# Rebuilding the head of a transformer-block kernel: modulation vector in column quarters, head 0's v, k, q accumulated feature by feature, one gate projection moved forward

## The chip, the cores and the metric

The kernel runs on one core of a Trainium2 chip. The metric is the device time of the whole program in microseconds (us), a median over runs. The engines are named as the profile names them: PE (TensorE; PEld is its weight load), DVE (VectorE), ACT (ScalarE), POOL (GpSimd) and SP (SyncE, which issues most DMAs).

## The reference

One layer of a diffusion block on 512 latent tokens and 256 context tokens, width 1024, one batch, all in float32. The core of it:

```python
mod_lat = jnp.split(jax.nn.silu(c) @ w_ada[l] + b_ada[l], 6, axis=-1)
mod_ctx = jnp.split(jax.nn.silu(c_ctx)[None, :] @ w_ada[l] + b_ada[l], 6, axis=-1)
...
pl = project(modulate(rmsnorm(x, g_mix[l]), sh1, sc1), w_in[l], w_dec_up[l], b_dec[l])
pc = project(modulate(rmsnorm(ctx, g_mix[l]), sh1c, sc1c), w_in[l], w_dec_up[l], b_dec[l])
o_c, s_cf, s_cb = gla_bidir(pc[0], pc[1], pc[2], pc[4], pc[5], zeros_state, zeros_state)
o_l, _, _ = gla_bidir(pl[0], pl[1], pl[2], pl[4], pl[5], s_cf, s_cb)
mix_l = merge_branches(o_l, pl[3], ...)          # o * silu(g), convolution branch, output projection
x = x + gt1[:, None, :] * mix_l
x = x + gt2[:, None, :] * swiglu(modulate(rmsnorm(x, g_ffn[l]), sh2, sc2), w_ffn_in[l], w_ffn_out[l])
return rmsnorm(x, g_final)
```

`project` multiplies by one matrix `w_in` whose columns are q, k (512 each), v, g (1024 each), a 32-column low-rank input `dd` for the decays, and the columns of the convolution and of the branch gates. There are 4 attention heads with 128 key and 256 value channels each. The change concerns the first of these steps: `mod` (shift and scale of the first norm, 2048 of the 6144 columns of `w_ada`), the modulated tokens, and the projections of head 0.

## The kernel before

Matmuls keep float32 accuracy by splitting each operand into a rounded part (`hi`) and the rest (`lo`) and adding three products; that is `mm3`, and L145 is the line on which all such matmuls are recorded. `split` makes the two parts: ACT casts `hi`, DVE subtracts for `lo`. The helper `Pinned` (L103) records most ACT and DVE work. A weight piece is loaded raw by SP's queue (tag `raw`, 4 buffers), then split.

PSUM has 8 banks: 3 are handed out as `bank`, 5 as `gbank`; a new tile of a name waits for the oldest one of its kind to be read out.

**The head before.** The modulation is a matrix-vector product for two vectors at once (`c2v`, latent and context). It is made in 8 pieces, one per 128-column feature tile f: shift and scale columns of f, so 256 output columns, stationary operand 2 columns wide, 8 float32 products over k, each of which the engine runs as two instructions of 256 columns (L279). For f = 3 and 6 (`ADA_SPLIT`) the weights are split first (L274). A row of 2 results is copied to SBUF, turned into columns by tiny matmuls (`adac`, L298), biased (`modT`, `gs`), and the feature of the normalised, transposed tokens is scaled and split (`mod_split`, L288 to L290). Tokens are normalised and transposed through PSUM (L251 to L261) between the pieces. Once all eight features exist, head 0's v is computed for the four latent token tiles (v, 256 columns, and dd, 32), then context tiles, k, the decays' inputs (`ddt`, z), q.

**The order.** Up to `pinned[0] = True` a scheduler orders the instructions of each engine from its own estimates; behind it, program order holds. From there on the numbers and letters of ORDER0, ORDER and ORDER3 set how many steps of filler matmuls stand between the attention steps of a head: `fill(n)` issues n steps. Heads 0 to 2 use the next head's v, k and q as filler; head 3 uses the g and branch-gate projections of all heads (`G_ORDER`). Each step is one mm3. `SPLITS` and `SPLITS3` are the step numbers at which the next weight unit is split and another one's load issued.

Of the kernel before, what the change touches and what calls it, by code (L numbers as in the profile page):

```python
# [23 lines left out]
H = 4  # L24
# [22 lines left out]
def hybrid_block(ctx: ExitStack, tc: tile.TileContext, x, c, ctxt, c_ctx, w_ada, b_ada, g_mix, w_in,  # L47
# [15 lines left out]
    ADA_SPLIT = (3,6)  # L63
# [79 lines left out]

    def mm(*a, **k):
        pin(nc.tensor.matmul(*a, **k))  # L145

    def tr(*a):
        pin(nc.tensor.transpose(*a))
# [18 lines left out]
    w_ada_v = w_ada[:, :2 * D].rearrange("(q a p) (s f) -> q p a s f", q=2, p=P, s=2)  # L167

    def ada_load(f):
        us = []  # L170
        for q in range(2):
            u = wp.tile([P, 4, 2, P], F32, tag="raw", name=f"r_wa{f}_{q}", bufs=4)
            for s_ in range(2):
                nc.sync.dma_start(u[:, :, s_, :], w_ada_v[q][:, :, s_, f * P:(f + 1) * P])
            us.append(u)
        return us

    wa = {0: ada_load(0)}
    ident = cst.tile([P, P], F32, name="ident")
    make_identity(nc, ident)  # L180
    eps = cst.tile([P, 1], F32, name="eps")
# [32 lines left out]
    c2v = c2.rearrange("p (s k) -> p k s", s=2)  # L214

    c4 = cst.tile([P, KT, 4], F32R, name="c4")
    nc.vector.tensor_copy(c4[:, :, 0:2], c2v)
    nc.vector.tensor_sub(c4[:, :, 2:4], c2v, f32(c4)[:, :, 0:2])
    sel = cst.tile([4, 2], F32, name="sel")
    nc.vector.tensor_add(sel, ident[0:4, 0:2], ident[0:4, 2:4])  # L220


    vrow = u2("vrow")
    vec = cst.tile([P, R_N], F32, name="vec")

    def small_vectors():
        for r0, src in ((R_GM, g_mix), (R_GF, g_ffn), (R_BA, b_ada), (R_GH, g_head)):
            n = src.shape[1] // P
            nc.sync.dma_start(vrow[r0:r0 + n, :P], src.rearrange("o (r f) -> (o r) f", f=P))
        nc.sync.dma_start(vrow[R_BD:R_BD + 8, :P], b_dec[0].rearrange("d (r f) -> (d r) f", f=P))  # L230
        nc.sync.dma_start(vrow[R_WC:R_WC + 24, :P], w_conv[0].rearrange("d (r f) -> (d r) f", f=P))
        vps = bank("vps")
        nc.tensor.transpose(vps[:, :R_N], vrow[:R_N, :P], ident[:R_N, :R_N])
        nc.vector.tensor_copy(vec, vps[:, :R_N])


    hp = tc.alloc_tile_pool(name="hp", bufs=1)
    xsT = hp.tile([P, KT, T], F32, name="xsT")
    xcT = hp.tile([P, KT, TC], F32, name="xcT")

    def tokens(i):
        src, dst, j = (x, xsT, i) if i < NT else (ctxt, xcT, i - NT)
        xt = hp.tile([P, D], F32, tag="xt", name=f"xt{i}", bufs=6)
        if i < NT:
            nc.sync.dma_start(xt, src[j * P:(j + 1) * P, :])
        else:
            with tc.issue_after(v_loads[-1].ins):
                nc.sync.dma_start(xt, src[j * P:(j + 1) * P, :])
        junk = hp.tile([P, D], F32, tag="jk", name=f"junk{i}", bufs=1)
        ss = sm.tile([P, 1], F32, tag="ss", name=f"ss{i}")  # L250
        nc.scalar.activation(junk, xt, AF.Square, accum_out=ss)  # L251
        r = rstd_of(ss, 1, D, f"x{i}")
        nc.vector.tensor_scalar_mul(xt, xt, r)
        for hh_ in range(2):
            tp = gbank(f"xtp{i}_{hh_}", (P, 4, P))
            for k in range(4):
                nc.tensor.transpose(tp[:, k, :], xt[:, (hh_ * 4 + k) * P:(hh_ * 4 + k + 1) * P], ident)
            if hh_ == 0:
                nc.scalar.copy(dst[:, :4, j * P:(j + 1) * P], tp)
            else:  # L260
                nc.vector.tensor_copy(dst[:, 4:, j * P:(j + 1) * P], tp)  # L261
# [3 lines left out]
    rows = {}  # L265

    def ada_rows(f):
        rows[f] = gbank(f"ada{f}")
        if f in ADA_SPLIT:
            for q in range(2):  # L270
                parts_ = split_raw(wa[f][q], f"wa{f}_{q}")
                for i, w_ in enumerate(parts_):
                    for k in range(4):
                        nc.tensor.matmul(rows[f][0:4, :256], c4[:, q * 4 + k, :], w_[:, k].rearrange("p s f -> p (s f)"),  # L274
                                         start=(q + i + k == 0), stop=(q + i == 2 and k == 3))
            return
        for q in range(2):
            for k in range(4):
                nc.tensor.matmul(rows[f][0:2, :256], c2v[:, q * 4 + k, :], wa[f][q][:, k].rearrange("p s f -> p (s f)"),  # L279
                                 start=(q + k == 0), stop=(q == 1 and k == 3))  # L280
# [5 lines left out]
    def mod_split(src, f, j, hi, lo):  # L286
        g_, sh = gs[:, f, j:j + 1], modT[:, f, 0, j:j + 1]
        nc.scalar.activation(hi, src[:, f, :], AF.Identity, scale=g_, bias=sh)  # L288
        nc.vector.tensor_scalar(src[:, f, :], src[:, f, :], g_, sh, ALU.mult, ALU.add)
        nc.vector.tensor_sub(lo, src[:, f, :], f32(hi))  # L290

    def modulate(f):
        n = 4 if f in ADA_SPLIT else 2
        rsb = sm.tile([4, 256], F32, tag="adar", name=f"adar{f}", bufs=2)
        nc.vector.tensor_copy(rsb[0:n, :], rows[f][0:n, :256])
        cp = gbank(f"adac{f}")
        for s_ in range(2):
            nc.tensor.matmul(cp[:, 2 * s_:2 * s_ + 2], rsb[0:n, s_ * P:(s_ + 1) * P], sel[0:n, :], start=True, stop=True)  # L298
        nc.vector.tensor_tensor(modT[:, f], cp[:, 0:4].rearrange("p (s c) -> p s c", s=2),
                                vec[:, R_BA + f:R_BA + f + KT + 1:KT].unsqueeze(2).broadcast_to([P, 2, 2]), ALU.add)  # L300

        nc.vector.scalar_tensor_tensor(gs[:, f, :], modT[:, f, 1, :], 1.0,
                                       vec[:, R_GM + f:R_GM + f + 1].broadcast_to([P, 2]), ALU.add, ALU.mult)
        mod_split(xsT, f, 0, *h[f])
# [16 lines left out]
    ada_rows(0)  # L321
    with tc.issue_after(silu_c.ins):
        tokens(0)
    tokens(1)
    wa[1] = ada_load(1)
    ada_rows(1)
    tokens(2)
    tokens(3)
    small_vectors()
    for f in range(2, KT):  # L330
        wa[f] = ada_load(f)
        ada_rows(f)
        modulate(f - 2)
        if f == 5:
            wdu_load()

# [22 lines left out]
    v_loads = []  # L359
    stv = [u2(f"st{i}", F32, (P, 4, P)) for i in range(2)]  # L360

    def v_slab(hd):

        n = HV + 32
        units = []
        per = 1024 // n
        for k in range(0, KT, per):
            e = min(k + per, KT)
            r = wp.tile([P, e - k, n], F32, tag="raw", name=f"r_v{hd}_{k}", bufs=4)
            nc.sync.dma_start(r[:, :, :HV], w_in[k * P:e * P, CV + hd * HV:CV + (hd + 1) * HV].rearrange("(a p) b -> p a b", p=P))  # L370
# [78 lines left out]


    v_slab(0)
    modulate(KT - 2)
    modulate(KT - 1)
    for i in range(NC_):
        tokens(NT + i)
# [634 lines left out]
```

## Time and profile before

| | before |
|---|---|
| median of 3 runs | 1024.05 us (1023.79 to 1024.25) |
| the profiled execution: its own time | 1025.91 us |
| span of that execution's trace | 1024.2 us |
| PE busy | 1003.4 us, 98% of the span |
| DVE busy | 549.2 us, 54% |
| ACT busy | 384.2 us, 38% |
| DMA, mean over the span | 114 GB/s |

Times in the rows are microseconds from the start of the span. In a row of the timeline or of the grouped view, the text before the arrow is what is written and the text behind it is what is read; x and a number is a count of instructions. Where a mean is given, it is in nanoseconds and is the duration of one instruction; on a pipelined engine neighbours overlap, so the pace of a long run is its length divided by its count.

### The profile page before, as it was taken

To read this page: it belongs to the slowest core of one execution; us is meant where nothing else is said; L and a number is where in the kernel's file an instruction comes from. 1 tells how busy PE (TensorE), PEld (TensorE's weight loads), DVE (VectorE), ACT (ScalarE), POOL (GpSimd) and SP (SyncE) were. 2 spreads that over 40 slices of the span, in tenths; PEclk is the share of its full clock that TensorE was granted. 3 is DMA by queue.
4 is the path that set the end of the run, shared out by engine and by line. 5 is a ranking of instruction groups with operands and counts; after the bars stand their busy time and mean duration, and the time that the engine had idled before them with its cause. 6 is when DMAs were issued, how large, how long until landed. Compare 5 with 4: busy or idle time off the path is not lost.

```text
span 1024.2 us, 13014 instructions
## 1 busy us (share of the span) xinstructions
PE 1003.4 (98%) x5270; PEld 833.4 (81%) x5274; DVE 549.2 (54%) x885; ACT 384.2 (38%) x594; POOL 6.2 (1%) x18
## 2 busy tenths in 40 slices
PE   6999999999999999999999999999999999999997
PEld 3598888888788888888888888888888888888886
DVE  4778876776536687778534445743332333322423
ACT  4547465558344322233123223642332322311223
POOL 2000000000000000000000000000000000000000
PEclk9999999999999999999999999999999999999999
DMA  8932112112326767666623322233233233232302
GB/s 250 272 113 62 41 43 62 35 50 62 104 71 181 211 179 200 196 195 213 199 83 97 106 86 83 83 104 103 82 104 102 83 109 97 84 127 77 124 21 83
DMA packets 117845, 117.16 MB, mean 114 GB/s; under 512 B 5415, under 2 KB 105881, under 8 KB 117785
## 3 DMA queue, kind: packets, MB, share of 16 engines
q1 hardware_dynamic: 117528, 116.07, 37.8%
q8 instruction: 41, 0.67, 0.3%
q0 software_dynamic: 256, 0.26, 0.1%
q14 instruction: 20, 0.16, 0.0%
HBM read 114.22 MB, written 2.10 MB: 114 GB/s over the span
## 4 chain that ended last, share of the span: by engine, by line
PE 92%; DVE 2%; ACT 2%; DMA 1%; issue 1%; SPq 0%; ACTq 0%
PE f L145 23%; PE fo L145 10%; PE v L145 5%; PE yc L145 4%; PE yg L145 4%; PE cb L145 4%; PE g L145 4%; PE ch L145 4%; PE cc L145 4%; PE gb L145 4%; PE ga L145 4%; PE mx L145 3%; PE kl L145 2%; PE o L145 2%; PE F L145 2%; PE q L145 2%
## 5 line engine op out<-in xcount | busy, mean ns | idle before, releaser
L145 PE MATMUL f<-h,h_fa 128*128 128x512 f32 (+1 forms) x384 | 111.0, 372 | 0.2 <-DVE h L103 0.2
L145 PE MATMUL f<-h,h_fb 128*128 128x512 f32 (+1 forms) x384 | 110.3, 372 | 0.0
L145 PEld LDWEIGHTS f<-h,h_fa 128*128 128x128 f32 x384 | 70.2, 188 | 13.3 <-DVE h L103 0.8
L145 PEld LDWEIGHTS f<-h,h_fb 128*128 128x128 f32 x384 | 70.0, 188 | 12.4
L145 PE MATMUL f<-h,l_fb 128*128 128x512 f32 (+1 forms) x192 | 71.3, 371 | 0.0
L145 PE MATMUL f<-h,l_fa 128*128 128x512 f32 (+1 forms) x192 | 71.3, 371 | 0.0
L103 DVE TENSOR_TENSOR l_fa<-r_fa,h_fa 128x1024 fp32r<-128x1024 f32 x22 | 26.9, 1225 | 74.6 <-ACT h_fa L103 74.6
L103 DVE TENSOR_TENSOR l_fo<-r_fo,h_fo 128x1024 fp32r<-128x1024 f32 x22 | 26.9, 1224 | 69.0 <-ACT h_fo L103 69.0
L145 PE MATMUL fo<-h_fo,ah 128*128 128x512 f32 x154 | 60.5, 393 | 0.0
L145 PE MATMUL fo<-l_fo,ah 128*128 128x512 f32 x154 | 60.5, 393 | 0.0
L145 PE MATMUL fo<-h_fo,al 128*128 128x512 f32 x154 | 60.4, 392 | 0.0
L807 DVE SCALAR_TENSOR_TENSOR acc<-r_wa,c,acc 128x256 f32<-128x256 f32 x112 | 54.1, 483 | 5.9 <-DMA r_wa<-in_w_ada_dram 3.0
L145 PE MATMUL v<-h_v,h 128*128 128x256 f32 (+1 forms) x256 | 51.3, 294 | 1.9 <-DVE vl L103 1.7
L103 ACT CAST h_fo<-r_fo 128x1024 fp32r<-128x1024 f32 x22 | 23.1, 1050 | 71.0 <-PE fo L145 27.4
L145 PEld LDWEIGHTS v<-h_v,h 128*128 128x128 f32 x256 | 41.9, 195 | 2.7 <-DVE vl L103 1.9
L145 PEld LDWEIGHTS f<-h,l_fb 128*128 128x128 f32 x192 | 36.2, 188 | 6.2
L145 PEld LDWEIGHTS f<-h,l_fa 128*128 128x128 f32 x192 | 36.1, 188 | 6.2
L145 PE MATMUL g<-h,h_g 128*128 128x512 f32 x128 | 39.9, 392 | 0.0
L145 PE MATMUL gb<-h,h_gb 128*128 128x512 f32 x128 | 39.8, 392 | 0.0
L145 PE MATMUL cb<-h,h_cb 128*128 128x512 f32 x128 | 39.7, 391 | 0.0
L145 PE MATMUL ch<-h,h_ch 128*128 128x512 f32 x128 | 39.6, 390 | 0.0
L145 PE MATMUL cc<-h,h_cc 128*128 128x512 f32 x128 | 39.6, 390 | 0.0
(276 smaller groups left out, 2275.5 us busy)
## 6 DMA issues: line engine op xcount, KB each, us to landing
r_wa<-in_w_ada_dram SPq DMA_DIRECT2D x32, 512.0 KB, 4.7
r_fa<-in_w_ffn_in_dram SPq DMA_DIRECT2D x22, 512.0 KB
r_fb<-in_w_ffn_in_dram SPq DMA_DIRECT2D x22, 512.0 KB, 3.5
r_fo<-in_w_ffn_out_dram SPq DMA_DIRECT2D x22, 512.0 KB, 3.6
r_wa<-in_w_ada_dram SPq DMA_DIRECT2D x32, 256.0 KB, 3.8
r_kq<-in_w_in_dram SPq DMA_DIRECT2D x16, 256.0 KB, 4.6
r_g<-in_w_in_dram SPq DMA_DIRECT2D x8, 512.0 KB, 3.8
r_gb<-in_w_in_dram SPq DMA_DIRECT2D x8, 512.0 KB
```

Source lines behind the costliest of these rows:

```text
L103: return lambda *a, **k: pin(getattr(self.engine, op)(*a, **k))
L145: pin(nc.tensor.matmul(*a, **k))
L807: nc.vector.scalar_tensor_tensor(acc, w_[:, k, :], ck, acc, ALU.mult, ALU.add)
```

## The change

The head is rewritten. The modulation is made in four quarters of two feature tiles each (shift and scale together 512 output columns). Its stationary operand `cw` is now 32 columns wide, 2 used and 30 zero. The eight products over k are spread over four groups of 32 output partitions (`g_ = 32 * (k % 4)`), so the groups sit in different columns of PE's array; `sel` then adds the four groups while it turns rows into columns. No piece is split any more. The loads come in whole 1-KB rows per column block instead of 512-byte rows.

Head 0's weights come in four pieces `w00` to `w03` of 256 input features with v, dd, k and q columns together (1088 values per partition). As soon as a feature tile k is modulated, its products are added to six open accumulators: four token tiles of v in `vo`, k in `ko`, q in `qo` (`gather_v`, `gather`). These hold all 3 `bank` and 3 of the 5 `gbank`. The context tokens are loaded, transposed and modulated between the seventh and the eighth feature; their v and k follow. SP issues all four token tiles first, then the first quarter, then w00. The small vectors go through POOL's queue. All of these matmuls are kept in program order (`pe_pin`).

Head 0's g projection (two tiles, 16 steps) leaves head 3's filler and stands between the head and the attention of head 0, with ddt, z and the decays among its steps; the multiplication by silu(g) is held back until the attention output exists (`gate`). Head 3's list `G_ORDER` and its split points are shortened to match.

```diff
-    def ada_rows(f):
-        rows[f] = gbank(f"ada{f}")
...
-                nc.tensor.matmul(rows[f][0:2, :256], c2v[:, q * 4 + k, :], wa[f][q][:, k].rearrange("p s f -> p (s f)"),
-                                 start=(q + k == 0), stop=(q == 1 and k == 3))
...
+    cw = hp.tile([P, KT, 32], F32, name="cw")
+    nc.vector.memset(cw, 0.0)
+    nc.vector.tensor_copy(cw[:, :, 0:2], c2v)
+    sel = hp.tile([P, 2], F32, name="sel")
+    nc.vector.tensor_add(sel, ident[:, 0:2], ident[:, 32:34])
+    nc.vector.tensor_add(sel, sel, ident[:, 64:66])
+    nc.vector.tensor_add(sel, sel, ident[:, 96:98])
...
+    def ada_rows(p_, us):
+
+        rows = gbank(f"ada{p_}")
+        for k in range(KT):
+            g_ = 32 * (k % 4)
+            mm(rows[g_:g_ + 32, :], cw[:, k, :], us[k // 2][:, k % 2].rearrange("p s f -> p (s f)"), start=k < 4, stop=k >= 4)
+        rsb = u2(f"adar{p_}")
+        nc.vector.tensor_copy(rsb, rows)
+        return rsb
...
+    def w0_load(p_):
+
+        r = hp.tile([P, 2, NW + 256], F32, tag="wr", name=f"r_w0{p_}", bufs=2)
+        for d0, c0, n in ((0, CV, HV), (HV, CD, 32), (NW, CK, P), (NW + P, CQ, P)):
+            nc.sync.dma_start(r[:, :, d0:d0 + n], w_in[p_ * 256:(p_ + 1) * 256, c0:c0 + n].rearrange("(a p) b -> p a b", p=P))
+        return r
...
+    def gather_v(os, src, k):
+        for i, o in enumerate(os):
+            mm3(o[:, :NW], tuple(w_[:, i * P:(i + 1) * P] for w_ in src[k]), w0_at(k, 0, NW), k == 0, k == KT - 1)
+
+    def gather(o, c0, src, k, n=T):
+        mm3(o[:, :n], w0_at(k, c0, c0 + P), tuple(w_[:, :n] for w_ in src[k]), k == 0, k == KT - 1)
...
+    xts = [token_load(i) for i in range(NT)]
+    was = {0: ada_load(0)}
+    wr = w0_load(0)
+    was[1] = ada_load(1)
...
+    for p_ in range(4):
+        k = 2 * p_
+        if p_ < 3:
+            wr = w0_load(p_ + 1)
+        if p_ < 2:
+            was[p_ + 2] = ada_load(p_ + 2)
...
+        gather_v(vo, h, k)
+        gather(ko, NW, h, k)
+        gather(qo, NW + P, h, k)
+        if p_ < 3:
+            rsb = ada_rows(p_ + 1, was[p_ + 1])
+        else:
+            for i in range(NC_):
+                tokens(NT + i, xts[i], xcT, i)
+            for f in range(KT):
+                mod_ctx(f)
+        gather_v(vo, h, k + 1)
+        if p_ < 3:
+            modulate(p_ + 1, rsb)
+            w0.append(split_raw(wr, f"w0{p_ + 1}"))
+        gather(ko, NW, h, k + 1)
+        gather(qo, NW + P, h, k + 1)
...
+    for k in range(3):
+        gather_v(vc, hc, k)
+    v_done(0, NC_, vo[0])
+    kc = bank("kc0")
...
+    for i in range(1, NT):
+        v_done(0, NC_ + i, vo[i])
+    for k in range(3, KT + 3):
+        if k < KT:
+            gather_v(vc, hc, k)
+        gather(kc, NW, hc, k - 3, TC)
...
-    G_ORDER = [("g", 0), ("g", 1), ("g", 2), ("gb", 0), ("gb", 1), ("g", 3), ("gb", 2), ("gb", 3)]
+    G_ORDER = [("g", 1), ("g", 2), ("gb", 0), ("gb", 1), ("gb", 2), ("g", 3), ("gb", 3)]
...
-    run(k_tile(0, True))
-    for _ in range(3):
-        next(stages[0]["A"])
-    run(q_tile(0))
-    run(stages[0]["A"])
...
+    fill(4, -1)
+    for i in range(NC_):
+        ddt(i)
+    for _ in range(2):
+        next(stages[0]["A"])
+    fill(5, -1)
+    next(stages[0]["A"])
+    fill(8, -1)
+    run(stages[0]["A"])
...
-    fill(129 - nwork, H - 1)
+    fill(113 - nwork, H - 1)
```

The order of ACT's instructions in the first part of the program, before the change. `xt` are raw token tiles, `rs` the root of their mean square, `xtp` their transposes in PSUM, `xsT` the transposed tokens, `h_wa`, `h_v` and `h_kq` the casts of weight pieces.

```order
L259 COPY xsT_128<-xtp0_0_156 128x4x128
L259 COPY xsT_128<-xtp1_0_177 128x4x128
L103 ACTIVATE rs_x2_209<-ss2_207,eps_84 128x1
L251 ACTIVATE junk3_227,ss3_228<-xt3_225 128x1024
L103 ACTIVATE rs_x3_230<-ss3_228,eps_84 128x1
L259 COPY xsT_128<-xtp2_0_213 128x4x128
L259 COPY xsT_128<-xtp3_0_234 128x4x128
L103 CAST h_wa3_0_287<-r_wa3_0_280 128x1024
```

The same place on ACT with the change:

```order
L251 COPY xsT_130<-xtp0_0_186 128x4x128
L102 ACTIVATE rs_x2_220<-ss2_218,eps_86 128x1
L102 ACTIVATE rs_x3_239<-ss3_237,eps_86 128x1
L102 CAST h_w00_281<-r_w00_161 128x1088
L251 COPY xsT_130<-xtp1_0_205 128x4x128
L251 COPY xsT_130<-xtp2_0_224 128x4x128
L251 COPY xsT_130<-xtp3_0_243 128x4x128
L102 CAST h_w01_377<-r_w01_306 128x1088
L288 ACTIVATE h0_133<-xsT_130,modT_131,gs_132 128x512 x2
```

Before, no weight cast stood ahead of the copies of the token tiles; now the cast of w00, which needs the piece's load, stands ahead of the copies of tiles 1, 2 and 3.

DVE at the same place with the change (`xtp1_1` is the second half of tile 1, `adar` the copied rows of the modulation):

```order
L102 TENSOR_TENSOR l_w00_282<-r_w00_161,h_w00_281 128x1088
L253 COPY xsT_130<-xtp1_1_211 128x4x128
L253 COPY xsT_130<-xtp2_1_230 128x4x128
L245 TENSOR_SCALAR xt3_147<-xt3_147,rs_x3_239 128x1024
L253 COPY xsT_130<-xtp3_1_249 128x4x128
L455 COPY vec_79<-vps_178 128x98
L279 COPY adar0_266<-ada0_257 128x512
L300 TENSOR_TENSOR modT_131<-adac0_268,vec_79 128x8
L303 SCALAR_TENSOR_TENSOR gs_132<-modT_131,vec_79 128x4
L102 TENSOR_TENSOR l_w01_378<-r_w01_306,h_w01_377 128x1088
L289 TENSOR_SCALAR xsT_130<-xsT_130,gs_132,modT_131 128x512 x2
L290 TENSOR_TENSOR h2_135<-xsT_130,h0_133 128x512 x2
```

And PE, which runs what stands here in order:

```order
L153 MATMUL xtp3_0_243<-ident_73,xt3_147 128x128 x4
L153 MATMUL xtp3_1_249<-ident_73,xt3_147 128x128 x4
L153 MATMUL vps_178<-ident_73,vrow_78 128x98
L150 MATMUL ada0_257<-wa00_149,cw_123 32x512 x2
L150 MATMUL ada0_257<-wa01_152,cw_123 32x512 x2
L150 MATMUL ada0_257<-wa02_155,cw_123 32x512 x2
L150 MATMUL ada0_257<-wa03_158,cw_123 32x512 x2
L150 MATMUL adac0_268<-sel_126,adar0_266 128x2 x4
L150 MATMUL v0_2_285<-h_w00_281,h0_133 128x288
L150 MATMUL v0_2_285<-l_w00_282,h0_133 128x288
L150 MATMUL v0_2_285<-h_w00_281,h2_135 128x288
```

The normalising multiplication of token tile 3 (`xt3`) now follows `l_w00` on DVE, the transposes of that tile follow the multiplication on PE, and the first quarter of the modulation follows those transposes.

The second place is ACT at the start of head 0's decays (`t1` is the softplus of the decays, made by two table functions one after the other; `sg0_0` and `sg0_1` are silu of head 0's g tiles). Before:

```order
L103 ACTIVATE t1_01_894<-z01256_900,vec_124 128x512
L103 ACT_TABLE_LOAD
L103 ACTIVATE t1_00_884<-t1_00_884 128x768
L103 ACTIVATE t1_01_894<-t1_01_894 128x768
L103 ACT_TABLE_LOAD
L103 ACTIVATE t1_00_884<-t1_00_884 128x768
L103 ACTIVATE t1_01_894<-t1_01_894 128x768
L103 CAST h_kq1_0_950<-r_kq1_0_840 128x1024
```

With the change:

```order
L102 ACT_TABLE_LOAD
L102 ACTIVATE sg0_0_884<-g0_0_821 128x512
L102 ACT_TABLE_LOAD
L102 ACTIVATE t1_00_843<-t1_00_843 128x768
L102 ACTIVATE t1_01_853<-t1_01_853 128x768
L102 ACT_TABLE_LOAD
L102 ACTIVATE sg0_1_913<-g0_1_886 128x512
L102 ACT_TABLE_LOAD
L102 ACTIVATE t1_00_843<-t1_00_843 128x768
L102 ACTIVATE t1_01_853<-t1_01_853 128x768
L102 CAST h_kq1_0_930<-r_kq1_0_811 128x1024
```

The silu of the second g tile, which needs the last of the moved g matmuls, stands ahead of the second function of both decays.

## Rows read from the trace of the kernel before

**Rows 1.** Busy time of PE in the whole span, from the page.

```profile
PE 1003.4 (98%) x5270; PEld 833.4 (81%) x5274; DVE 549.2 (54%) x885; ACT 384.2 (38%) x594; POOL 6.2 (1%) x18
```

**Rows 2.** Chain that ended last, first 140 us: start, length, what.

```profile
21.49 1.90 PE xtp L257 x16
...
35.28 1.83 PE ada L279 x8
...
46.33 0.98 PE adac L298 x8
...
61.46 9.78 PE v L145 x72
71.24 5.48 PE kl L145 x24
...
77.54 2.88 PE kc L145 x24
```

**Rows 3.** What PE waited for, first 100 us: total, times, longest.

```profile
PE ada L279 <- DMA r_wa<-in_w_ada_dram: 4.0, 3, 2.7
PE xtp L257 <- DVE xt L253: 3.4, 2, 3.1
```

**Rows 4.** Timeline of PE and DVE around head 1's first v tiles: start, busy, what.

```profile
86.44 0.28 PE L145 MATMUL v<-h_v,hc 128*128 128x256 f32 x1
96.91 0.39 PE L145 MATMUL v<-h_v,h 128*128 128x256 f32 x1 [1.67 <-DVE vl L103]
...
90.51 0.93 DVE L103 TENSOR_TENSOR la<-t,la 128x768 f32<-128x768 f32 x1
91.48 1.76 DVE L103 TENSOR_TENSOR_SCAN b<-smask,la 128x768 f32<-128x768 bf16 x1
```

**Rows 5.** Windows: length, busy of engines, then granted clock, DMA share, GB/s.

```profile
2.50:17.50 15.00, 8.76 (x35) 4.15 (x36) 5.64 (x21) 4.28 (x9) 5.47 (x12) 0.94 1.00 298
20.00:45.00 25.00, 23.71 (x135) 11.66 (x134) 18.84 (x41) 10.53 (x14) 0.00 (x0) 1.00 0.95 272
...
343.00:346.00 3.00, 3.00 (x15) 2.49 (x14) 0.35 (x1) 1.05 (x2) 0.00 (x0) 1.00 1.08 366
```

**Rows 6.** Page, DMA issues: KB each, us from issue to landing.

```profile
r_fb<-in_w_ffn_in_dram SPq DMA_DIRECT2D x22, 512.0 KB, 3.5
```

**Rows 7.** Instructions grouped by shape, first 100 us: busy, mean ns, idle before.

```profile
L288 ACT ACTIVATE h<-xsT,modT,gs 128x512 fp32r<-128x512 f32 x8 | 6.5, 813 | 7.3 <-DVE gs L302 7.2
...
L290 DVE TENSOR_TENSOR h<-xsT,h 128x512 fp32r<-128x512 f32 x8 | 5.5, 690 | 0.1
L103 ACT ACT_TABLE_LOAD x4 | 5.1, 1283 | 0.1
L103 DVE TENSOR_TENSOR l_wa<-r_wa,h_wa 128x1024 fp32r<-128x1024 f32 x4 | 4.9, 1214 | 0.1
L253 DVE TENSOR_SCALAR xt<-xt,rs_x 128x1024 f32<-128x1024 f32 x6 | 4.5, 752 | 0.2
L289 DVE TENSOR_SCALAR xsT<-xsT,gs,modT 128x512 f32<-128x512 f32 x8 | 4.3, 532 | 1.0 <-ACT h L288 0.9
L103 ACT CAST h_wa<-r_wa 128x1024 fp32r<-128x1024 f32 x4 | 4.2, 1046 | 4.5 <-DMA r_wa<-in_w_ada_dram 4.5
...
L290 DVE TENSOR_TENSOR hc<-xcT,hc 128x256 fp32r<-128x256 f32 x8 | 3.2, 418 | 0.0
...
L261 DVE COPY xsT<-xtp 128x512 f32<-128x512 f32 x4 | 2.7, 686 | 1.2 <-PE xtp L257 1.0
```

**Rows 8.** Windows around PE's granted clock, columns as in group 5.

```profile
15.50:19.00 3.50, 3.50 (x14) 1.67 (x13) 1.27 (x2) 1.54 (x4) 0.00 (x0) 0.51 0.53 192
...
46.00:49.70 3.70, 3.70 (x25) 3.10 (x24) 2.99 (x8) 3.22 (x5) 0.00 (x0) 1.00 0.95 304
49.70:53.10 3.40, 3.40 (x17) 3.40 (x16) 3.37 (x9) 3.37 (x7) 0.00 (x0) 0.50 1.08 322
```

**Rows 9.** A 40-ns window, attention scores F only: 32-column matmuls in four array columns.

```profile
102.80:102.84 0.04, 0.04 (x8) 0.04 (x8) 0.00 (x0) 1.00 0.00 0
```

## What the change does to the time, from the trace of before

> **What bounds the kernel now.** First the engine table: PE is busy 98% of the span [rows 1], so a change pays where it takes work or waits from PE, and costs where it makes PE wait. Next the chain that ended last, for the first 140 us: nearly all of it is PE, one block behind the other [rows 2]. PE's idle time there is small: 4.0 us for the modulation weights, 3.4 us for token tiles that DVE had not normalised [rows 3], and 1.7 us ahead of head 1's fourth v tile, for DVE's `vl` [rows 4]. So before, the first 45 us are full, but of work with 2-column stationary operands, beside which loads run at 272 GB/s [rows 5]. The new head takes most of that work away, and its weights, copies and casts then decide when PE can start.
>
> I compare at one mark: the start of head 1's v tile that follows the 1.7 us wait, 96.91 [rows 4]. What stands behind it is the same in both, except that 48 matmuls of g (16 steps of three) are now ahead of it instead of in head 3. At 5.48/24 = 0.228 us [rows 2] they are 10.9 us. Head 3's fill is dense PE work, so it gets 10.9 us shorter; its shifted split points I cost at nothing, for casts and loads lie under that work; without the cover one cast and one subtraction, 2.3 us [rows 7], would show. So the result is the new mark, less 10.9, less 96.91.
>
> **A. The load of w00.** Ahead of it and with it SP's queue carries 2.10 MB of tokens, 2.10 MB of the first quarter and 0.56 MB of w00: 4.75 MB. Before, loads ran at 272 to 298 GB/s in stretches with 512-byte rows and at 366 with longer ones [rows 5]. The new rows are mixed (tokens 4 KB, quarter 1 KB, k and q 512 bytes), so I take 325: 14.6 us from 2.5. Landing adds about 2.1, for a 512-KB load takes 3.5 [rows 6], of which 1.4 are transfer at 366. It lands at 19.2; the bounds are 17.6 (366) and 22.1 (272).
>
> The Trainium skill ("DMA: Bandwidth & Descriptors", Specifications) puts line rate at transfers of 512 bytes and more. By it longer rows bring nothing, w00 lands at 22.1 and the sum is 2.9 us higher (rival 5). The trace speaks against it, 272 to 366, though those two stretches differ in more than row length.
>
> **B. To the first product.** The order shows a queue in front of it: ACT's cast of w00 stands ahead of the copies of tiles 1 to 3, DVE's `l_w00` ahead of its copies and of tile 3's multiplication. Durations are scaled to 1088 values from [rows 7]: cast 1.1, `l_w00` 1.3, two copies 1.4, multiplication 0.75, then eight transposes at 1.90/16 = 0.12 [rows 2], 1.0: 24.8. The modulation quarter costs 2.1 warm: 16 instructions of 512 columns at twice 1.83/8 [rows 2] are 7.3 in a row, 1.8 in four groups at once, and 0.3 for changing array shapes (my guess; nothing and 1 are the bounds). That the groups overlap, the attention scores show: eight 32-column matmuls are in flight in the same 40 ns [rows 9]. But PE has idled, and before the granted clock was 0.51 at 15.50 to 19.00 [rows 8], behind the 3.1 us wait of [rows 3]: this is the level of 1.2 GHz. So 3.6 instead of 2.1: 28.4. Then the row copy 0.7, eight `adac` at 0.98/8 [rows 2] 1.0, the small DVE operations 0.3, `l_w01` 1.3, two scalings 1.06, one subtraction 0.7 [rows 7]: 33.5. Before, v began at 47.3 [rows 2].
>
> The rule on this overlap is in the Trainium skill ("TensorEngine Tiling (Array Packing)", Overview): column tiles of 32 work as independent small arrays, up to four times as fast. It would give the quarter the same 1.8 us.
>
> **C. Four quarters.** For a feature, v costs 12 x 9.78/72 = 1.63 and k with q 6 x 0.228 = 1.37 [rows 2]. Per quarter: even feature 3.0, next modulation 2.1, odd v 1.63, `adac` 1.0, odd k and q 1.37. The next lo part is ready 2.45 after `adac` (small operations 0.3, then ACT's scaling 0.81, DVE's scaling 0.53 and subtraction 0.69 [rows 7], and 0.1 of hand-over), and only k, q and two products cover it: wait 0.8. That is 9.9 a quarter. Quarter 1 also starts cold, 1.7 more, as a 3.4 us stretch at 0.50 costs half [rows 8]. Feature 6 begins at 64.9 and ends at 67.6. The context's 16 transposes take 1.9 and 0.4 of waiting, since only two `gbank` are free; feature 7 ends at 72.9.
>
> **D. Context and kc.** DVE copies the context at 70.7, then scales and subtracts eight features, each two operations of the 0.42 of [rows 7], some 0.66 as neighbours overlap: 76.0. `kc0` needs the bank of the first v tile, whose last read is queued behind this on DVE and behind the scaling of q (0.69, like a copy of its size [rows 7]) and short operations, in all about 1.45 by estimate: 77.4. PE has four features of context v to cover it (3.3 us) and waits 1.2. Then four features of v, 24 x 0.136, and k, 24 x 0.12 [rows 2]: 83.6.
>
> **E, F. g of head 0.** ACT's cast of g's first half stands behind the copy of kc: copy and hand-over 0.6 (an estimate), cast 1.05, then DVE's subtraction 1.2 [rows 7]: third matmul at 86.4, a wait of 2.5. The rest of 48, 10.5, and about 1.4 for ddt and z (ten instructions at 0.12, and changes of shape) bring head 1's first v to 98.3; before it was 86.44 [rows 4], so with the 10.9 moved it is 1.0 late.
>
> **G. The decays.** The silu of g's second tile now stands ahead of the second softplus function on ACT, and it needs the last g matmul. From 98.3: silu 0.8 and one function 0.85 (both near ACT's 0.81 of [rows 7]), a table load of 1.28 between them [rows 7], `la` 0.93 and scan 1.76, and both again for the other direction [rows 4]: 106.6. From the end of the second scan to the mark was 96.91 - 93.24 = 3.67 [rows 4]: 110.3. PE's three v tiles end at 107.1: a wait of 3.2 in place of 1.7.
>
> **Sum.** 110.3 - 10.9 - 96.9 = +2.5 us on the profiled execution's 1025.91, so 1028.4; that execution stood 1.86 above the median. On the median of 1024.05 this is 1026.5. PE's modulation work falls by some 20 us; nothing before 24.8 for PE to do but transposes, and 10 us of short waits, eat it. POOL's six small loads cost nothing: their rows are needed only at the transposition ahead of the first quarter, 10 us later; uncovered, they move everything by their lateness.
>
> **The rivals.** What measurement can tell from no change is about 0.2%, 2 us.
> 1. *PE is not cold behind its idle time.* The first quarter takes 2.1, not 3.6, and quarter 1 loses no 1.7: 3.2 less, 1023.3, not slower. It decides once 2.5 of the 3.2 are not lost. For it: the granted clock was 0.94 over 2.50 to 17.50 with PE busy 8.76 of 15 us [rows 5]. Against it: [rows 8]. With w00 at 366 GB/s, 1021.7.
> 2. *The waits behind the gather are shorter.* D, E and G hold 6.9 us of waits that rest on my reading of two queues. If half: 1023; if nearly none: 1019.5.
> 3. *The quarters' gaps also lower the clock.* Before, a stretch of `adac` among v, 46.00 to 49.70, was followed by 3.4 us at 0.50 [rows 8]; each quarter has such a stretch. Three more: 3 x 1.7 = 5.1, so 1031.6. Against it: from 20.00 to 45.00 `adac` stood among other work too, and the clock was 1.00 [rows 5].
> 4. *The four groups do not overlap.* 7.3 instead of 2.1, four times: +21, 1047. Against it: [rows 9].
> 5. *Longer rows load no faster than before.* At 272 GB/s [rows 5] w00 lands at 22.1, 2.9 later, and so does all behind it: 1029.4. A quarter's 2.66 MB then take 9.8, just under the 9.9 of C. For it: the loads of a head are many and small; against it: the 366 of the same rows. This is also the case of the rule of the Trainium skill named in A.
>
> **Chances.** My forecast, 1023.5 to 1029.5: 0.36, half of it within 0.2% and half above. Rival 1: 0.24, about half under 1022 and half within 0.2%. Rival 2: 0.13, nearly all under 1022. Rivals 3, 5 and 4: 0.15, 0.07 and 0.05, all slower. So faster 0.25, same 0.31, slower 0.44. The range of 8 in 10 goes from 1019.5 (rival 2 in full) to 1031.5; it leaves out rival 4, half of rival 3 and some 0.04 below.
>
> **What would show it.** In the new trace: `h_w00` cast near 19.2; first modulation quarter at 24.8 with a granted clock of 0.5; first v at 33; quarters 9.9 apart; waits of PE ahead of kc, g and head 1's fourth v tile of 1.2, 2.5 and 3.2; head 1's first v at 98.3. I am wrong if the clock stays at 1.00 there, if quarters come 8 or 12 us apart, or if a modulation quarter takes 7 us.

## The result: slower by 0.84%, with its profile

| | before | after |
|---|---|---|
| median | 1024.15 us (1023.79 to 1024.7, 4 runs) | 1032.38 us (1032.13 to 1034.5, 4 runs) |
| ratio, 95% interval | | 1.0084 (1.0067 to 1.0102) |
| span of the profiled execution | 1024.2 us | 1030.4 us |
| PE busy in it | 1003.4 us, 98% | 990.1 us, 96% |

The change takes 13 us of busy time from PE, and yet the time rises by 8.2 us: PE waits more than it saves. The direction was forecast, with a chance of 0.44, the largest of the three; the size was not: 1026.5 was forecast, with a range to 1031.5.

The waits of PE in the first 130 us of the changed kernel, each with its total, count and longest. Before there were 4.0, 3.4 and 1.7 us [rows 3, 4].

```profile
PE xtp L153 <- DVE xt L245: 16.0, 2, 8.7
PE v L150 <- DVE h L290: 3.4, 4, 1.1
PE v L150 <- DVE vl L102: 3.3, 1, 3.3
...
PE kc L150 <- DVE st L102: 1.6, 1, 1.6
PE v L150 <- ACT h L288: 1.4, 1, 1.4
...
PE g L150 <- ACT h_g L102: 1.0, 1, 1.0
...
PE g L150 <- DVE l_g L102: 0.5, 1, 0.5
```

The modulation weights, for which PE waited before, are gone from the list; nearly every entry now names an ACT or DVE operation. The first, 16.0 us for the normalised token tiles, is made of 7.3 us before any tile is there and the 8.7 us that the next view explains. It is the chain that ended last in the changed kernel (start, length, what), which answers to [rows 2].

```profile
13.21 5.87 DMA r_w<-in_w_in_dram
19.15 1.11 ACT h_w L102
...
21.49 1.28 DVE xsT L253 x2
22.77 0.67 DVE xt L245
23.58 1.94 PE xtp L153 x8
25.68 2.79 PE ada L150 x16
...
38.34 1.85 PE ada L150 x16
...
48.34 1.85 PE ada L150 x16
...
90.70 9.10 PE g L150 x39
...
100.44 1.28 ACT L102
...
111.68 7.14 PE v L150 x45
```

Read it from the top. The piece w00 lands at 19.15, ACT casts it, DVE subtracts, then copies two token tiles, multiplies the fourth, PE transposes it, and only then, at 25.68, does the first modulation quarter run. The mark of the prediction, head 1's fourth v tile, is at 111.68.

Windows of the changed kernel (length, busy time of the engines, then granted clock, DMA share, GB/s) show where PE ran at 1.2 GHz for all or part of the time, and that it did not between 38 and 111.

```profile
20.00:24.00 4.00, 0.42 (x2) 0.46 (x3) 3.15 (x4) 1.22 (x3) 0.00 (x0) 0.50 1.10 349
...
33.60:38.00 4.40, 4.40 (x16) 3.96 (x16) 3.08 (x6) 0.00 (x0) 0.00 (x0) 0.55 1.08 330
38.00:111.00 73.00, 64.14 (x418) 52.14 (x416) 42.74 (x103) 35.82 (x55) 0.00 (x0) 1.00 0.36 109
111.68:115.00 3.32, 3.32 (x19) 3.32 (x20) 3.32 (x7) 3.32 (x9) 0.00 (x0) 0.64 0.18 52
...
111.68:118.98 7.30, 7.30 (x46) 7.03 (x46) 6.44 (x11) 5.12 (x12) 0.00 (x0) 0.77 0.08 24
```

The first two were expected: PE had idled, and the first gathered feature then ran at half pace. The last two were not: behind the 3.3 us wait the 46 instructions from the mark to the first scores took 7.30 us. In the kernel before, the same work behind its wait of 1.67 us took 5.81:

```profile
96.91:102.72 5.81, 5.65 (x45) 5.54 (x46) 5.81 (x10) 5.02 (x12) 0.00 (x0) 1.00 0.09 27
```

Last, the scores of all heads, with their count, shortest, median and longest duration, and first and last start, before and after:

```profile
L145 PE MATMUL F<-q,k x320: 196/219/270, 102.7 to 261.6; 128*32 128x64 f32 x64, 128*32 128x32 f32 x64, 128*64 128x64 f32 x32
```

```profile
L150 PE MATMUL F<-q,k x320: 196/219/270, 119.0 to 278.9; 128*32 128x64 f32 x64, 128*32 128x32 f32 x64, 128*64 128x64 f32 x32
```

From first to last scores it takes 159.9 us, and 158.9 before.

The difference of the two spans, 6.2 us, adds up from these marks. To the first scores the change costs 119.0 - 102.7 - 10.9 = 5.4 us, of which 111.68 - 96.91 - 10.9 = 3.9 lie ahead of the mark and 1.5 behind it; the heads cost 1.0; the rest gains 0.2.

### The profile page after: what moved, and what is told of

Read it like the earlier page. It is cut to its first block, busy times and chain, and to the rows that moved or that the text cites. A ratio compares the mean times of both kernels' runs of the same rounds, so it can differ in the third digit from the quotient of the medians.

```text
span 1030.4 us, 12875 instructions
## 1 busy us (share of the span) xinstructions
PE 990.1 (96%) x5210; PEld 827.5 (80%) x5210; DVE 545.0 (53%) x870; ACT 381.7 (37%) x591; POOL 10.0 (1%) x24
## 4 chain that ended last, share of the span: by engine, by line
PE 89%; DVE 5%; ACT 3%; DMA 1%; issue 1%; SPq 0%; DVEq 0%; ACTq 0%
PE f L150 23%; PE fo L150 10%; PE v L150 5%; PE yc L150 4%; PE yg L150 4%; PE gb L150 4%; PE cb L150 4%; PE ch L150 4%; PE cc L150 4%; PE ga L150 4%; PE g L150 4%; PE mx L150 3%; PE kl L150 2%; PE F L150 2%; PE fo1l L150 2%; PE o L150 1%
## 5 line engine op out<-in xcount | busy, mean ns | idle before, releaser
L150 PE MATMUL v<-h_v,h 128*128 128x256 f32 x192 | 38.0, 293 | 3.3 <-DVE vl L102 3.3
L150 PE MATMUL ga<-h,h_ga 128*128 128x512 f32 x128 | 39.5, 390 | 0.0
```

What stands on the lines that cost most here:

```text
L150: pe_pin(nc.tensor.matmul(*a, **k))
```

## The experiments

### 1. The casts of w0 behind the tokens

`split_behind` issues a piece's cast and subtraction behind a given ACT and a given DVE instruction.

```diff
-    w0.append(split_raw(wr, "w00"))
+    w0.append(split_behind(wr, "w00", tok["act"], tok["dve"]))
...
+            prev = dict(last)
             modulate(p_ + 1, rsb)
-            w0.append(split_raw(wr, f"w0{p_ + 1}"))
+            w0.append(split_behind(wr, f"w0{p_ + 1}", prev["act"], prev["dve"]))
```

> The changed kernel, but the casts and subtractions of the four w0 pieces are queued behind the work of the stage before them: w00 behind the last copies of the token tiles on ACT and DVE, w01 to w03 behind the scaling of the features already under way. Theory QUEUE: in the changed kernel PE idles until 25.6 us because the copies of tiles 1 to 3 and the multiplication of tile 3 stand behind w00, which lands at 19.15. Then the first modulation quarter starts near 16 instead of 25.6, the first full product of v near 25.7 instead of 33.6 (now w00 itself, its subtraction and the modulation chain are what is last), and the time falls by 6 to 8.5 us, to 1024 to 1026.5. Rival LOADS: the arrival of the weights sets the head's pace anyway; then the next quarters wait for w01 and the second modulation quarter, and the gain is under 3 us, 1029.5 or more.

1026.16 us (1024.98 to 1026.62), ratio to before 1.0016 (1.0007 to 1.0025): 6.2 us less than the changed kernel. PE's timeline (start, busy, what, and in brackets the idle time before it and its releaser):

```profile
16.04 2.41 PE L150 MATMUL ada<-wa,cw 128*32 128x512 f32 x16
22.39 1.87 PE L150 MATMUL adac<-sel,adar 128*128 128x2 f32 x8 [3.94 <-DVE adar L285]
...
26.92 0.85 PE L150 MATMUL v<-h_w,h 128*128 128x288 f32 x2 [0.46 <-DVE h L296]
```

The quarter starts at 16.04 in place of 25.68, as the theory of the queue said. Of the 9.6 us some are left in a new wait of 3.94: on DVE w00's subtraction now stands ahead of the row copy, and through it that copy waits for w00's cast (19.31) and so for w00's load. The rival, by which the next quarters would wait for their loads and less than 3 us be gained, falls: no wait of PE for a load of weights is in this trace.

### 2. g of head 0 back in head 3

```diff
-    G_ORDER = [("g", 1), ("g", 2), ("gb", 0), ("gb", 1), ("gb", 2), ("g", 3), ("gb", 3)]
+    G_ORDER = [("g", 0), ("g", 1), ("g", 2), ("gb", 0), ("gb", 1), ("g", 3), ("gb", 2), ("gb", 3)]
...
-    fill(4, -1)
...
-    fill(8, -1)
     run(stages[0]["A"])
```

> The changed head, but g of head 0 goes back into head 3's filler (list, split points and step count of before), and the decays follow the head directly. Theory COVER: the moved g covers part of the chain from z to the first scaled keys, about 16 us long in the kernel before; without it PE has only three v tiles (8.7 us) for it, the mark (head 1's fourth v tile) comes at about 103.3 instead of 111.68 - 10.9 = 100.8, its wait grows from 3.3 to about 7, and the time rises by 2.5 us to about 1035. Rival COST: moving g costs time by itself (silu ahead of the second softplus function, table loads, the wait for its cast); then undoing it gains about 2 us, 1030.

1037.14 us (1037.01 to 1038.64), ratio 1.0129 (1.0114 to 1.0144): 4.8 us more than the changed kernel, where 2.5 were expected. The moved g is cover, not cost. Two waits of PE in this run, then the chain that ended last just ahead of z, and a window:

```profile
89.11 1.01 PE L150 MATMUL z<-ddT,wdu 64*128 64x256 f32 x4 [2.95 <-DVE ddT L421]
105.93 0.58 PE L150 MATMUL v<-h_v,h 128*128 128x256 f32 x1 [4.58 <-DVE vl L102]
```

```profile
87.44 1.22 DVE l_v L102
88.66 0.41 DVE ddT L421 x2
...
89.11 0.59 PE z L150 x2
```

```profile
90.00:93.40 3.40, 3.40 (x17) 3.35 (x16) 2.29 (x4) 3.37 (x6) 0.00 (x0) 0.50 0.72 249
```

The mark is at 105.93 in place of the 103.3 expected. From the start of z to the mark it is 16.8 us, near the 16 assumed, but z itself starts at 89.11, where 103.3 less 16 is 87.3: on DVE the last two `ddT` stand behind `l_v`, the subtraction for head 1's weights, and PE waits 2.95 us for them, where g left a wait of 0.56 in the changed kernel. PE also runs at a granted clock of 0.50 behind that wait, but this does not move the mark: DVE's `vl` releases it, and the wait of 4.58 takes the slow stretch up.

### 3. Softplus before silu

```diff
-        act_.activation(t, o, AF.Silu)
...
+        if hd == 0:
+            late.append((j, o))
...
     run(stages[0]["A"])
+    for j, o in late:
+        silu_gate(0, j, o)
```

`silu_gate` makes the silu of one g tile; for head 0 both are now issued behind the decays.

> The changed kernel, but both silu of head 0's g stand behind the second softplus function of the decays on ACT. Theory SILU: the wait of 3.26 us ahead of head 1's fourth v tile is there because the second function waits for the last g matmul; it goes, and with it the 1.5 us that PE loses at a granted clock of 0.64 behind it: 4.8 us less, 1027.6. Rival CHAIN: the chain from z on is as long without the silu, so less than 1.5 us is gained (1031 or more).

1028.81 us (1027.24 to 1029.51), ratio 1.0041 (1.0027 to 1.0056): 3.6 us less. The wait ahead of head 1's fourth v tile is gone from the list, and the granted clock is 1.00 from 90 on. In the profiled execution the first scores are at 115.7, 3.3 earlier, though its second modulation quarter is at 39.89 in place of 38.27, 1.6 late. Its start ran longer at half clock; the first quarter shows it, in the changed kernel and then here:

```profile
25.61 2.72 PE L150 MATMUL ada<-wa,cw 128*32 128x512 f32 x16
```

```profile
25.81 3.64 PE L150 MATMUL ada<-wa,cw 128*32 128x512 f32 x16
```

With the 1.6 taken off the edit gives 4.9 in the profile, where 4.8 were expected; in the medians, whose executions vary by as much, it gives 3.6.

### 4. One column group

```diff
-            g_ = 32 * (k % 4)
-            mm(rows[g_:g_ + 32, :], cw[:, k, :], us[k // 2][:, k % 2].rearrange("p s f -> p (s f)"), start=k < 4, stop=k >= 4)
+            mm(rows[0:32, :], cw[:, k, :], us[k // 2][:, k % 2].rearrange("p s f -> p (s f)"), start=k == 0, stop=k == KT - 1)
...
```

The row copy then takes 32 rows only, and `adac` needs no adding of groups (`ident` in place of `sel`).

> The changed kernel, but all eight products of a modulation quarter go to the same 32 output partitions, one behind the other, instead of four groups. If the four groups run at the same time, a quarter takes 16 instructions of 512 columns at 0.46, 7.3 us, in place of 1.9 (2.7 for the first), and the time rises by 4 x 5.4 = 21 us or a little more for the first, cold one: about 1054. If they did not overlap, it would stay at 1032.

1052.72 us (1052.68 to 1052.76, 2 runs), ratio 1.0277 (1.0257 to 1.0298). The second quarter in its timeline:

```profile
42.52 7.05 PE L150 MATMUL ada<-wa,cw 128*32 128x512 f32 x16
```

It takes 7.05 us against 1.9 with four groups: they do overlap, by a factor of 3.7. The time is 20.3 us above the changed kernel, where 21 were expected.

### 5. The kernel before, once more

> The kernel before, unchanged, for a second profile. Its first profiled execution was 1.86 us above the median of its runs and shows two stretches at half the granted clock, 15.50 to 19.00 and 49.70 to 53.10. Theory CLOCK: the usual execution lacks the second stretch, which costs 1.7 us; then its span is near 1022.4 with PE's mean granted clock at 0.998 in place of 0.996. Rival: the usual span is 1024.2 too and the 1.9 us lie outside it.

1024.56 us (1023.73 to 1024.86, 8 runs); its profiled execution had 1024.66, and its span was 1023.0. The window that stands in [rows 8] with a clock of 0.50, in this execution:

```profile
49.70:53.10 3.40, 3.40 (x26) 3.39 (x26) 3.36 (x10) 3.37 (x8) 0.00 (x0) 1.00 1.08 334
```

These are 26 instructions in place of 17 in the same 3.4 us. The start of head 0's v and a later instruction of it, in the first profile and then in the second:

```profile
47.24 0.67 PE L145 MATMUL v<-h_v,h 128*128 128x288 f32 x3
...
61.46 0.37 PE L145 MATMUL v<-h_v,h 128*128 128x288 f32 x1 [0.21 <-DVE ddh L103]
```

```profile
47.73 0.67 PE L145 MATMUL v<-h_v,h 128*128 128x288 f32 x3
...
60.27 0.37 PE L145 MATMUL v<-h_v,h 128*128 128x288 f32 x1 [0.21 <-DVE ddh L103]
```

Between the two it is 14.2 us in the first and 12.5 in the second: the stretch at half clock cost 1.7, as expected. The span is only 1.2 shorter because v began 0.5 later. All of that lies ahead of the mark, which is at 95.71 here. The spans of the 23 executions timed with it were 1022.0 to 1024.1, most of them 1022.5 to 1023.3; the execution from which I took my rows, at 1024.2, is longer than all of them, and its extra lay in the very stretch that I compared.

### 6. Both repairs together

The edits of experiments 1 and 3.

> Both edits together: the w0 casts behind the token copies and the scaled features, and both silu of head 0's g behind the second softplus function. They act on different waits (PE before the first modulation quarter, PE before head 1's fourth v tile), so if both readings hold, the gains add: 1026.2 - 3.6 = 1022.6, between 1021.5 and 1023.5, a little faster than the kernel before. If the second wait was partly caused by the first, more than 1024.

1021.68 us (1021.32 to 1023.76), ratio 0.9975 (0.9963 to 0.9987). The gains add (10.7 us below the changed kernel, against 6.2 and 3.6 for each alone), and the kernel is now faster than before by 0.25%.

### 7. Row copy first

The kernel of experiment 6, with w00's subtraction behind the last small operation of the first quarter on DVE (`gs`).

```diff
-    w0.append(split_behind(wr, "w00", tok["act"], tok["dve"]))
+    w0.append(split_behind(wr, "w00", tok["act"], last["gs"]))
```

> The kernel with both edits, and the subtraction for w00 on DVE now behind the small operations of the first modulation quarter instead of ahead of its row copy. With the casts moved, PE waited 3.94 us for that copy (16.0 + 2.4 to 22.39). Theory QUEUE: adac comes near 19.5 in place of 22.4, the first full product near 23.6 in place of 26.9, and the time falls by about 3 us to 1019.6. Rival LOADS: the second quarter's weights and w01, landing near 25 and 27, are now last, and less than 1 us is gained.

1018.92 us (1018.19 to 1019.43), ratio 0.9944 (0.9929 to 0.9959): 2.8 us less than experiment 6, as the theory of the queue said. The first `adac`:

```profile
19.76 1.05 PE L150 MATMUL adac<-sel,adar 128*128 128x2 f32 x8 [0.89 <-DVE adar L285]
```

It comes at 19.76 (19.5 expected), behind a wait of 0.89 in place of 3.94.

### 8. PE kept busy in its idle time

The kernel of experiment 7, with matmuls of zeros (`spin`).

```diff
+    idle = bank("idle")
+    def spin(n):
+        for _ in range(n):
+            mm(idle, zeros[:, :P], zeros, start=True, stop=True)
+    spin(30)
     for i in range(NT):
         tokens(i, xts[i], lat, i)
...
     rsb = ada_rows(0, was[0])
+    spin(3)
     modulate(0, rsb)
+    spin(6)
```

> The kernel of the run before, with 39 extra matmuls of zeros into a PSUM bank that nothing reads: 30 ahead of the first transposes, 3 and 6 in the gaps around the first adac. They do no work of the reference and fill PE's idle time only. Theory CLOCK: PE's granted clock fell to 0.5 behind that idle time and the first gather products ran at half pace; with the gaps filled it stays at 1.00 and 1.5 to 2.5 us are gained, to 1017 to 1018.5. Rival: the cold stretch lies under waits for DVE and loads, and nothing is gained, or the extra matmuls cost their own time: 1019.5 or more.

1018.68 us (1018.3 to 1020.02), ratio 0.9947 (0.993 to 0.9963): no gain that can be told from none. First the window behind the idle time and the second quarter without the zeros, then with them.

```profile
24.10:29.30 5.20, 5.18 (x16) 4.21 (x16) 1.50 (x2) 1.10 (x1) 0.00 (x0) 0.50 1.14 332
```

```profile
29.37 2.09 PE L150 MATMUL ada<-wa,cw 128*32 128x512 f32 x16
33.09 0.95 PE L150 MATMUL adac<-sel,adar 128*128 128x2 f32 x8
```

```profile
24.10:29.30 5.20, 5.14 (x35) 3.17 (x36) 0.61 (x2) 1.03 (x1) 0.00 (x0) 1.00 1.11 329
```

```profile
27.06 1.92 PE L150 MATMUL ada<-wa,cw 128*32 128x512 f32 x16
31.69 1.05 PE L150 MATMUL adac<-sel,adar 128*128 128x2 f32 x8 [0.92 <-DVE adar L285]
```

The zeros did what they were meant to: the clock is 1.00 in place of 0.50, and PE reaches the second quarter 2.3 us earlier. At its `adac` 1.4 of that is left, for a new wait of 0.92 stands there. Half of the rest goes behind it: on DVE `modT` also stands behind four operations that prepare the decay weights (`wdu`, 31.55 to 33.78) and starts at 33.82, only 0.7 ahead of the 34.49 without zeros. Those four stand in the same place in experiments 1, 7 and 9, though `wdu` is first read by z; no run moves them. My theory was right on the clock and wrong on the time.

### 9. w01 behind the scale

The kernel of experiment 8, with w01's subtraction behind the second quarter's `gs`.

```diff
-            w0.append(split_behind(wr, f"w0{p_ + 1}", prev["act"], prev["dve"]))
+            w0.append(split_behind(wr, f"w0{p_ + 1}", prev["act"], last["gs"] if p_ == 0 else prev["dve"]))
```

> The kernel kept busy with zeros, and the subtraction for w01 on DVE now behind the small operations of the second quarter. Keeping the clock at 1.00 brought PE 1.4 us ahead at the second modulation quarter, of which 0.9 went into a new wait of adac for the row copy, because w01's subtraction, ahead of that copy on DVE, waits for w01's load. Theory: with that wait gone the gain of the clock arrives, 0.7 to 1.4 us less than 1018.7, about 1017.6. Rival: the wait only moves on to w01's products, and nothing is gained.

1017.43 us (1016.8 to 1019.44), ratio 0.9936 (0.9918 to 0.9954). The wait is gone:

```profile
30.31 0.95 PE L150 MATMUL adac<-sel,adar 128*128 128x2 f32 x8
```

The medians say 1.2 less than experiment 8, as expected, though the two ranges overlap. It is the fastest kernel of the study.

### 10. PE kept busy in the wait for `vl`

```diff
+            if hd == 1 and i == 3 and k == 0:
+                idle = gbank("idle")
+                for _ in range(14):
+                    mm(idle, zeros[:, :P], zeros, start=True, stop=True)
```

> The changed kernel with 14 extra matmuls of zeros on PE ahead of head 1's fourth v tile, in the 3.26 us in which PE waits for DVE. They belong to nothing in the reference. Theory CLOCK: behind that wait 7.3 us of work up to the first scores took 1.5 us more than the same work before, at a granted clock of 0.64; with PE busy in the wait the clock stays at 1.00 and the time falls by about 1.5 us, to 1030.9. Rival: the loss behind the wait is the next waits of DVE and ACT, not the clock; then nothing changes, 1032.4.

1031.19 us (1030.8 to 1032.4), ratio 1.0067 (1.0049 to 1.0085): 1.2 us less than the changed kernel, or 2.0 when from each the kernel before is taken that was timed beside it (1024.97 here); 1.5 were expected. From the mark to the first scores:

```profile
112.28:118.09 5.81, 5.81 (x46) 5.54 (x46) 5.81 (x10) 5.02 (x12) 0.00 (x0) 1.00 0.10 31
```

The same 46 instructions, in 5.81 us at a clock of 1.00 where the changed kernel took 7.30 at 0.77. The loss behind the wait is the clock's, and the wait itself stays.

### 11. The gates of head 0 in head 3

```diff
-            if i < len(og):
+            if i < len(og) and (i > 1 or len(og) >= 6):
```

> The changed kernel, but the two multiplications of head 0's output by silu(g) wait until head 3's g tiles, where they stood before; g itself stays moved. From the first to the last scores it took 159.9 us with g moved and 159.1 without (158.9 before). Theory GATE: these 0.8 to 1.0 us are the two multiplications, 0.7 each on DVE at the end of head 0, where DVE is late; the time falls by 0.8 us, to 1031.6, and first to last scores take 159.1. Rival: they come from elsewhere, and nothing changes.

The two multiplications of head 0's output by silu(g) wait until head 3 here. 1032.89 us (1032.61 to 1033.46), ratio 1.0082 (1.0066 to 1.0098): no gain in the median. The scores in its profile:

```profile
L150 PE MATMUL F<-q,k x320: 196/219/271, 120.3 to 279.3; 128*32 128x64 f32 x64, 128*32 128x32 f32 x64, 128*64 128x64 f32 x32
```

First to last is 159.0, so 0.9 us are won there, as expected. But the first scores come 1.3 later: in this execution the second quarter started at 39.48 in place of 38.27, and the median does not show 0.9 us in a head whose start varies by more. The profiles do: from first to last scores it is 159.8 to 159.9 us in all nine that have the two multiplications at the end of head 0, and 158.9 to 159.2 in the five that do not, the two of the kernel before among them. In the changed kernel they stand on DVE ahead of head 1's operands (156.39, 1.28 us), and PE waits 0.51 us for DVE within head 1's scores, at 165.57; in this run it does not.

### 12. The repaired head without the moved g

The edits of experiments 1, 2 and 7.

> The changed head with both repairs of its order (casts behind tokens and features, row copy first), but with g of head 0 in head 3's filler as before. If the parts add: 1037.1 for the head without the moved g, less 6.2 and 2.8 for the repairs, 1028.1: slower than before by 0.4%, so the moved g is needed as cover for the chain of the decays. Rival: the repaired head alone is already faster than before, under 1022, and the moved g is not what counts.

1028.91 us (1027.7 to 1029.02), ratio 1.0037 (1.0023 to 1.0051). Even repaired, the head is slower than before without g behind it, as expected (1028.1). PE waits 5.77 us for `vl` at the mark, where it waited 1.67 before [rows 4]:

```profile
97.30 0.58 PE L150 MATMUL v<-h_v,h 128*128 128x256 f32 x1 [5.77 <-DVE vl L102]
```

The head's PE work has become shorter than the chain of the decays, which has nothing else to lie under.

## Why the prediction was right in direction and wrong in size

**Right.** The steps A to C came out nearly as worked out: w00 cast at 19.15 (19.2), transposes of the last tile at 23.58 (about 23.8), first quarter at 25.68 (24.8), first full product at 33.59 (33.5), quarters 10.0 apart (9.9), a quarter 1.85 warm (2.1). Of the 0.3 guessed in it for changing array shapes at most 0.2 is seen: a quarter of experiment 4's 7.05 is 1.76, and the timeline gives 1.92 for four groups.

Two of these agreements are in part luck. The 325 GB/s of A came out as an average only, 407 over 4.00 to 6.00 and 291 over 16.00 to 18.00, shortly before w00 lands. And the first quarter began 0.9 late but took 2.79 in place of 3.6, at a granted clock of 0.75 over 25.60 to 29.00 and not 0.5.

The order of ACT and DVE is the cause of the late start: experiments 1 and 7 move nothing but the casts and subtractions of w0 and gain 6.2 and 2.8 us. The waits ahead of kc, g and the v tile were 1.6, 1.5 and 3.3 (1.2, 2.5, 3.2), and G's reason for the last one, silu ahead of softplus, is shown by experiment 3. Rival 1 is excluded by the windows at 0.50 and 0.55, rival 2 by these waits (6.4 in place of 6.9), rival 4 by experiment 4, rival 5 by w00's landing and by 349 GB/s in the window at 20: loads with 1-KB rows ran faster than the 272 of [rows 5].

The Trainium skill ("TensorEngine Tiling (Array Packing)", Overview) gives up to 4 times for a dimension of 32 or less; experiment 4 measured 3.7. The Trainium skill's line-rate rule ("DMA: Bandwidth & Descriptors", Specifications: transfers of 512 bytes and more) would by the prediction's estimate have had w00 land at 22.1; it landed at 19.15, and the measurement decides.

**Wrong: the base of the sum.** I worked out 1028.4 against an execution of 1025.91, and carried the difference over to the median of 1024.05. But that execution's own excess lay in the compared stretch, as experiment 5 shows: the half-clock stretch at 49.70 to 53.10, which the second profile lacks, cost 1.7. I had its row and used it as rival 3, not as a correction. Of the missing 5.9 us the base is 2.0: the medians differ by 8.2, the spans by 6.2, since the profiled execution of the kernel before lies 1.8 above its median and that of the changed kernel 0.25 below.

**Wrong: the clock behind the wait in G.** I priced the wait of 3.2 us at 3.2. It also cost 1.5 us behind it, at a granted clock of 0.64 in the 3.3 us that followed; experiment 10 takes just that away. [Rows 8] showed what a wait of 3.1 us is followed by, and I had applied it in B and not in G. Rival 3 had the mechanism, but named the wrong gaps: between the quarters the clock stayed at 1.00, so that its 1031.6 lies near the result by luck.

**Wrong: small terms, nearly all of one sign.** Feature 7 ended 0.6 later than worked out and kc began 0.5 later still; z waited 0.56 for DVE, which I had not priced. With small gains between, head 1's v began 1.3 late, at 99.62 in place of 98.3, and the mark was at 111.68 in place of 110.3. The length of the chain from there to the mark was right (12.1 in place of 12.0). The two gate multiplications cost some 0.9 between the first and last scores, which I had not priced at all: it goes in the trace of experiment 11 and is absent with g back in head 3 (113.2 to 272.3, 159.1). The wait of 0.51 in head 1's scores is a part of it; where the rest arises is open, and no median shows it.

So 2.5 + 1.4 + 1.5 + 0.9 are 6.3, near the difference of the spans (6.2); the base adds the other 2.0.

## What to carry to other kernels

When a rewrite shortens an engine's own work, the next bound is the order in which the other engines' queues hand it its inputs: look for the instruction that waits for the last load, or the last matmul, and stands ahead of ones whose inputs are long there. Here moving three such groups (experiments 1, 3 and 7) turned +0.84% into -0.56%. And before an execution's rows become the base of a sum, check that its excess over the median does not lie in the stretch that is compared; a wait of some 3 us amid dense work, as here, is then priced with the half-clock stretch behind it, unless the next wait takes that up anyway (as in experiments 2 and 8; in experiment 10 it did not).

## What was not expected of the hardware

In the middle of the kernel PE's granted clock fell behind the long waits and not behind the short ones. A wait of 1.67 us left it at 1.00, one of 2.95 (experiment 2) was followed by 0.50, one of 3.3 by 0.64, and 14 matmuls of zeros in that last wait kept it at 1.00. But neither does every long wait bring such a stretch nor every stretch need a wait. The first 7.3 us wait of the changed kernel, ahead of its first transposes, was followed by 1.00 from 10.00 to 16.00. And in the 30 us ahead of 49.70 in the kernel before, PE waited at most 0.82 us at a time, and the second profile lacks the stretch. What decides in these cases is open.

Where such stretches fall also moves the same program from one execution to the next. With the same instructions ahead of it, the second modulation quarter of the changed head started at 38.27 (the changed kernel), 38.37, 38.80, 39.48 and 39.89 (experiments 2, 10, 11 and 3), and the first quarter took 2.72, 2.52, 2.90, 3.34 and 3.64 us in them. It is not shown that the clock makes all of the scatter of whole executions: of the 44 of the kernel before that were timed beside the experiments, the eight with a mean granted clock of 0.999 had spans of 1021.7 to 1023.9, and the twelve with 0.996 had 1022.0 to 1024.1.
